# Hybrid DeltaNet / GLA / softmax layer on one core: GLA projections traced a pair ahead of the mixing, and a DeltaNet block inverse that is masked before its elimination

## The chip, the core and the metric

One NeuronCore of a Trainium2 chip runs the whole program. The metric is device time in microseconds (us), the median of several executions. Engines are named as in the profile: PE is TensorE (matmul), PEld its weight load, DVE is VectorE, ACT is ScalarE, POOL is GpSimd, SP is SyncE; a "q" behind a name is the engine's instruction queue issuing a DMA. Each engine works through its own list of instructions in order, so an instruction that waits holds up everything behind it on that engine.

## The reference, cut to what matters

A layer over 528 positions (16 meta tokens and 512 tokens) of width 2048: an RMS norm, one wide input projection, three token mixers on separate heads, an output projection, a residual sum and a last norm. The two mixers that the change touches:

```python
# gated DeltaNet, 6 heads of 128, chunks of 64; the kernel uses chunks of 128
a_mat = where(strict_lower, einsum(kb, kc) * decay, 0)
sol = triangular_solve(eye + a_mat, rhs)          # unit lower triangular
...
# GLA, 5 heads, key width 64: decay per key channel inside the score
attn = einsum('bhid,bhjd,bhijd->bhij', q_c, k_c, exp(g_i - g_j))   # i >= j
o = einsum(qd, s) + einsum(attn, v_c)
s = s * g_last + einsum(kd, v_c)
```

All of it is float32. Large matmuls split each operand into a rounded part and a remainder and sum three products.

## The kernel before

**The stream of projections.** `inproj` (L188) computes one block of 128 projection columns: two weight halves are loaded by SP, split by ACT (`whi`, L144) and DVE (`wlo`, L145), and each half feeds 48 matmuls of 264 or 258 columns or 24 of 512 (L174), with the two-deep buffers `raw`, `hi`, `lo`. The third product needs `wlo`, so DVE has to reach L145 before PE gets to the half. PE's 4368 such matmuls form one stream, in a fixed order, and everything else PE does is put between them.

**Who sets the order.** The program is traced in the order of the source, and a scheduler with a timeline of its own then orders every engine's list. Two things steer it by hand: `tc.high_priority(...)`, which moves what is traced inside ahead of what is ready at the same time (it is used for the weight splits, L143), and `behind(mm, n)` (L162), which ties a matmul behind the n-th projection matmul from the one last traced.

**DeltaNet.** For each group g of three heads (L885 to L892) the keys are projected (`dn_keys`), then values, queries, the inverse and the mixing. `dn_keys` forms the matrices `an` from `pg` (keys times keys), `e2` (the decays: DVE L434, ACT L435) and per-row factors (DVE L438). `dn_inverse` (L443) writes the 32-by-32 diagonal blocks of `an` through DRAM into `ab`, one block per partition (51 rows of 1024), eliminates with 60 DVE instructions (L463, L465), then selects the strict lower triangle and puts ones on the diagonal with two POOL instructions (L466, L468), and writes `ab` out (`sc`, L471) and back as `xc` (`iv`, L474), both issued by ACT. DVE transposes it (L479). PE then builds the inverse of the whole block in two steps: 32-row products `pm` and `pl` (L485, L494, L495) with copies by ACT (`m1` L489, `l1` L496) and DVE (`uf` L504), and 64-row products `pn` and `pu` (L515, L520). The first `pm` of each group is tied `PM[g]` = 308 or 310 projection matmuls behind the point where it is traced; `pn` has no tie.

**GLA.** `gla_pair` (L648) treats pair p (two heads for p = 0, 1, one for p = 2): it projects keys, queries and values, scans the log gates (`gu`, `gt`, `gc`; L669 to L676), computes the scores on eight levels of block size 64, 32, ..., 1, 0 (DVE L695 to L703, ACT L698, PE `pss` L717), copies them into place (L721, L725) or under a mask (DVE L729), and then runs the state and the output (`pkd` L742, `pg` L760, `pgn` L768, `pgo` L777, L783, `pgt` L797). PE writes `pss`, `pkd` and nearly all other small results to the four PSUM buffers of the tag "m"; a level's buffers come free when L721, L725 or L729 has read them. With two heads a level is 32 small matmuls (64 weight columns by 32), so two levels are a burst of 64.

Of the kernel before, what the change touches and what calls it, by code (L numbers as in the profile page):

```python
# [14 lines left out]
ALU = mybir.AluOpType  # L15
# [12 lines left out]
H = 3  # L28
# [49 lines left out]
def tile_hybrid_trunk(ctx, tc, xT, xtok, mtok, w_gate, w_in, w_out, consts, lmask, fin_w, out, dbg=None):  # L78
# [20 lines left out]
    V, A, G, PE = nc.vector, nc.scalar, nc.gpsimd, nc.tensor  # L99
# [62 lines left out]
    def behind(mm, n):  # L162

        later.append((mm.ins, len(order) + n))
# [85 lines left out]
    for b in range(5):  # L250
        r = NM if b == 4 else P
# [9 lines left out]
    for b in range(5):  # L261
        r = NM if b == 4 else P
# [55 lines left out]
    for k in range(KT):  # L318
        for xx in (xh, xl):
            for a in range(2):  # L320
                PE.matmul(pgate[a][:, :HT], wg[k // 8][:, k % 8, :], xx[k][:, a * HT : (a + 1) * HT],
                          start=(k == 0 and xx is xh), stop=(k == KT - 1 and xx is xl))
# [52 lines left out]
    def dn_keys(g):  # L375

        st = {}
        hs = range(H * g, H * g + H)
        kT = six.tile([P, H, T], F32, tag="six", name=f"kT{g}")
        for j, h in enumerate(hs):  # L380
            conv_silu(("dk", h), 6 + h, kT[:, j])
        gb = six.tile([P, H, T], F32, tag="six", name=f"gb{g}")
        nc.scalar.dma_start(out=gb, in_=gd[6 + H * g : 6 + H * g + H, :].partition_broadcast(P))
        kd = six.tile([P, NN, P], F32, tag="six", name=f"kd{g}")
        at = six.tile([P, NN, P], F32, tag="six", name=f"at{g}")
        an = six.tile([P, NN, P], F32, tag="six", name=f"an{g}")
        sk = wk.tile([P, 5, H], F32, tag="sk", name=f"sk{g}")
        kdm = t15(f"kdm{g}", (NM, H, P))
        anm = wk.tile([NM, H, NM], F32, tag="anm", bufs=1, name=f"anm{g}")
        atm = wk.tile([NM, H, NM], F32, tag="atm", bufs=1, name=f"atm{g}")  # L390
        cols = wk.tile([P, 4, 5, H], F32, tag="cols", name=f"cols{g}")
        nb2, br, nbg, tmp = (cols[:, i] for i in range(4))
        gcl = lambda b, j: gcol[:NM if b == 4 else P, b, 6 + H * g + j : 6 + H * g + j + 1]
        G.memset(sk, 1.0)
        for b in (4, 0, 1, 2, 3):
            r = NM if b == 4 else P
            ts = slice(0, NM) if b == 4 else bsl(b)
            pk = psm.tile([P, 512], F32, tag="m", name=f"pk{g}{b}")
            for j in range(H):
                PE.transpose(pk[:r, j * P : (j + 1) * P], kT[:, j, ts], ident)  # L400
            for j in range(H):
                sq = wk.tile([P, P], BF16, tag="sq", name=f"sqk{g}{b}{j}")
                A.activation(sq[:r], pk[:r, j * P : (j + 1) * P], AF.Square, accum_out=sk[:r, b, j : j + 1])
            e = at[:, b * H : b * H + H, :] if b < 4 else atm
            for j in range(H):
                V.tensor_scalar(e[:r, j, :], gb[:r, j, ts], gcl(b, j), 0.0, ALU.subtract, ALU.min)
            A.activation(e, e, AF.Exp)
            for j in range(H):
                dst = kd[:, b * H + j, :] if b < 4 else kdm[:, j, :]
                V.tensor_scalar_mul(dst, pk[:r, j * P : (j + 1) * P], e[:r, j, r - 1 : r])  # L410
            if b < 4:
                G.affine_select(out=e, in_=e, pattern=[[0, H], [1, P]], base=0, channel_multiplier=-1,
                                compare_op=ALU.is_ge, fill=0.0)
        A.activation(tmp, sk, AF.Ln, bias=eps_c)
        A.activation(br, tmp, AF.Exp, scale=-0.5)
        lb = gcol[:, :, H * g : H * g + H]
        gg = gcol[:, :, 6 + H * g : 6 + H * g + H]
        for sl, r in ((slice(0, 4), P), (slice(4, 5), NM)):
            c = lambda t: t[:r, sl, :]
            A.activation(c(tmp), c(lb), AF.Exp)  # L420
            V.tensor_tensor(out=c(nb2), in0=c(tmp), in1=c(br), op=ALU.mult)
            V.scalar_tensor_tensor(out=c(tmp), in0=c(nb2), scalar=-1.0, in1=c(br), op0=ALU.mult, op1=ALU.mult)
            V.tensor_copy(c(br), c(nb2))
            V.tensor_copy(c(nb2), c(tmp))
            A.activation(c(nbg), c(gg), AF.Exp)
            V.tensor_tensor(out=c(nbg), in0=c(nbg), in1=c(nb2), op=ALU.mult)
        for b in (4, 0, 1, 2, 3):
            r = NM if b == 4 else P
            ts = slice(0, NM) if b == 4 else bsl(b)
            pg = psm.tile([P, 512], F32, tag="m", name=f"pg{g}{b}")  # L430
            e2 = t15(f"e2{g}{b}")
            for j in range(H):
                PE.matmul(pg[:r, j * r : (j + 1) * r], kT[:, j, ts], kT[:, j, ts], start=True, stop=True)
                V.tensor_scalar(e2[:r, j, :r], gb[:r, j, ts], gcl(b, j), 0.0, ALU.subtract, ALU.max)  # L434
            A.activation(e2[:r, :, :r], e2[:r, :, :r], AF.Exp, scale=-1.0)  # L435
            for j in range(H):
                dst = an[:, b * H + j, :] if b < 4 else anm[:, j, :]
                V.scalar_tensor_tensor(out=dst, in0=pg[:r, j * r : (j + 1) * r], scalar=nb2[:r, b, j : j + 1],  # L438
                                       in1=e2[:r, j, :r], op0=ALU.mult, op1=ALU.mult)
        st.update(kT=kT, kd=kd, at=at, an=an, kdm=kdm, anm=anm, br=br, nbg=nbg)  # L440
        return st

    def dn_inverse(g, st):  # L443
        an, anm = st["an"], st["anm"]
        ab = six.tile([NN * 4 + H, 1024], F32, tag="six", name=f"ab{g}")
        G.memset(ab, 0.0)
        scr = drp.tile([NN * 4, 1024], F32, tag="scr", name=f"scr{g}", bufs=2)
        for r in range(4):
            nc.scalar.dma_start(
                out=scr.rearrange("(n r) (a c) -> r a n c", r=4, a=32)[r],  # L450
                in_=an[32 * r : 32 * r + 32, :, 32 * r : 32 * r + 32])
# [3 lines left out]
        nc.scalar.dma_start(  # L455
            out=ab[NN * 4 : NN * 4 + H, :].rearrange("h (a c) -> h a c", a=32)[:, 0:NM, 0:NM],
            in_=scm_.rearrange("a h c -> h a c"))
        a3 = ab.rearrange("p (a c) -> p a c", a=32)
        for j in range(1, 31):
            m = 31 - j  # L460
# [2 lines left out]
            V.tensor_tensor(out=t3, in0=a3[:, j + 1 :, j : j + 1].to_broadcast([NN * 4 + H, m, j]),  # L463
                            in1=a3[:, j : j + 1, 0:j].to_broadcast([NN * 4 + H, m, j]), op=ALU.mult)
            V.tensor_tensor(out=a3[:, j + 1 :, 0:j], in0=a3[:, j + 1 :, 0:j], in1=t3, op=ALU.add)  # L465
        G.affine_select(out=a3, in_=a3, pattern=[[1, 32], [-1, 32]], base=0, channel_multiplier=0,  # L466
                        compare_op=ALU.is_gt, fill=0.0)
        G.affine_select(out=a3, in_=a3, pattern=[[1, 32], [-1, 32]], base=0, channel_multiplier=0,  # L468
                        compare_op=ALU.not_equal, fill=1.0)
        sc2 = drp.tile([NN * 4 + H, 1024], F32, tag="sc2", name=f"sc2{g}", bufs=2)  # L470
        nc.scalar.dma_start(out=sc2, in_=ab)  # L471
        iv = six.tile([P, 4, NN, 32], F32, tag="six", name=f"iv{g}")
# [9 lines left out]
        for n in range(NN):  # L482
            for q in range(2):
                lo_, hi_ = slice(64 * q, 64 * q + 32), slice(64 * q + 32, 64 * q + 64)
                mm = PE.matmul(pm[lo_, n, :], an[hi_, n, lo_], uc[hi_, n, :], start=True, stop=True)  # L485
# [12 lines left out]
        uf = six.tile([P, NN, P], F32, tag="six", name=f"uf{g}")  # L498
# [6 lines left out]
        for q in range(2):  # L505
            ns = range(q * 6, q * 6 + 6)
            nsl = slice(q * 6, q * 6 + 6)
            b64 = t15(f"b64{g}{q}", (64, 6, 64))
            G.memset(b64, 0.0)
            V.tensor_copy(b64[0:32, :, 0:32], xc[0:32, nsl])  # L510
            V.tensor_copy(b64[32:64, :, 32:64], xc[32:64, nsl])
            V.tensor_copy(b64[32:64, :, 0:32], l1[32:64, nsl])
            pn = psm.tile([64, 6, 64], F32, tag="m", name=f"pn{g}{q}")
            for n in ns:
                PE.matmul(pn[:, n - q * 6, :], an[64:128, n, 0:64], uf[64:128, n, 64:128], start=True, stop=True)  # L515
            m2 = t15(f"m2{g}{q}", (64, 6, 64))
            A.copy(m2, pn)
            pu = psm.tile([64, 6, 64], F32, tag="m", name=f"pu{g}{q}")
            for n in ns:
                PE.matmul(pu[:, n - q * 6, :], b64[:, n - q * 6, :], m2[:, n - q * 6, :], start=True, stop=True)  # L520
            V.tensor_copy(uf[0:64, q * 6 : q * 6 + 6, 64:128], pu)
# [123 lines left out]

    kts, qts, ats = [], [], []

    def gla_pair(p):  # L648
        R = P if p < 2 else 64
        ne = 2 if p < 2 else 1  # L650
        qk = six.tile([P, 3, T], F32, tag="six", name=f"gqk{p}")
        kT, qT, gc = qk[:R, 0], qk[:R, 1], qk[:R, 2]
# [7 lines left out]
        vt = six.tile([P, 2, S], F32, tag="six", name=f"gvt{p}")  # L660
        vm = t15(f"gvm{p}", (NM, 2, P))
# [12 lines left out]
        A.activation(t, t, AF.Ln, bias=1.0)  # L674
        V.scalar_tensor_tensor(out=u, in0=u, scalar=0.0, in1=t, op0=ALU.min, op1=ALU.subtract)
        V.tensor_tensor_scan(gc, gsc[:R], u, 0.0, ALU.mult, ALU.add)  # L676
        SC = 1.0 / 16.0
        k4, q4, g4 = (a[:, NM:].rearrange("p (b t) -> p b t", b=NB) for a in (kT, qT, gc))
        n_n = ne * NB
# [220 lines left out]
    kts += [kq[0][:, :S], kq[0][:, S : 2 * S]]  # L900
    qts += [kq[0][:, 2 * S :], kq[1][:, :S]]
    ats.append(kq[1][:, S:].rearrange("p (n t) -> p n t", t=P))
    for p in range(3):
        gla_pair(p)
    for h in range(GLA_HEADS):
        dump(f"ogl{h}", zs["gz", h])
    for h in range(FOX_HEADS):
# [176 lines left out]
```

## Time and profile before

| | us |
|---|---|
| median of 3 runs | 1032.09 (1031.01 to 1033.81) |
| the profiled execution | 1035.39 |
| its span, first to last instruction | 1033.7 |
| PE busy in the span | 1011.4 (98%) |
| DVE, ACT, POOL busy | 566.7, 411.7, 136.4 |
| mean granted clock of PE in the span | 0.992 |

The profile's page gives busy time by engine, the chain of work that ended last, and groups of instructions by line. The waits of an engine list how long it stood idle and what ended the idle time. The table by stretches gives busy time inside chosen windows, with the granted clock of PE (PEclk, 1.00 is full speed). The timeline lists instructions with start, duration, engine, line and tile, and in brackets the idle time ahead of one and what ended it. A busy PE can still be a slow one, since a busy matmul at half the clock is busy too.

### The profile page before, as it was taken

What the parts mean: (1) busy time and instruction counts of PE and PEld (TensorE: products, weight loads), DVE (VectorE), ACT (ScalarE), POOL (GpSimd) and SP (SyncE); (2) the same over time, 40 slices, a digit from 0 to 9 for tenths busy, and PEclk for the clock granted to TensorE, in tenths of its full rate; (3) what the DMA queues carried; (4) which work ended last, traced back from release to release, by engine and by line L of the source; (5) the groups of instructions that cost most, each with busy time, mean ns of one, the idle gap of its engine ahead of it and who ended that gap; (6) DMA issues with size and microseconds to landing.
All of it is one profiled execution on the core that took longest, in us unless ns stands there. A gap on an engine that the chain in (4) does not pass through costs nothing.

```text
span 1033.7 us, 19032 instructions
## 1 busy us (share of the span) xinstructions
PE 1011.4 (98%) x7799; PEld 910.3 (88%) x7799; DVE 566.7 (55%) x1240; ACT 411.7 (40%) x899; POOL 136.4 (13%) x137
## 2 busy tenths in 40 slices
PE   9999999999999998999989999999999999999996
PEld 7899999989999888899989879898998988888885
DVE  6366868856577883243747474445454574423234
ACT  6644533343455343243444444343333353213223
POOL 0022212221122222100101010110101010000014
PEclk9999999999999998999999999999999999999998
DMA  9613232323222233132112122222232254222244
GB/s 354 239 62 115 83 90 91 102 78 108 78 83 81 78 102 99 49 94 74 62 48 83 44 92 66 91 82 92 82 93 82 93 193 133 82 100 85 102 142 163
DMA packets 42347, 105.15 MB, mean 102 GB/s; under 512 B 10589, under 2 KB 13917, under 8 KB 42260
## 3 DMA queue, kind: packets, MB, share of 16 engines
q1 hardware_dynamic: 28000, 92.33, 26.3%
q10 hardware_dynamic: 14260, 11.61, 4.1%
q8 instruction: 61, 1.00, 0.4%
q14 instruction: 26, 0.21, 0.1%
HBM read 98.74 MB, written 5.05 MB: 100 GB/s over the span
## 4 chain that ended last, share of the span: by engine, by line
PE 66%; DVE 5%; DMA 3%; issue 3%; ACT 2%; POOL 1%; ACTq 0%; POOLq 0%; DVEq 0%
PE pp L174 39%; PE pa L932 15%; DMA sc<-ab 1%; PE pss L717 1%; POOL stgz L294 1%; DVE wlo L145 1%; PE pfo L877 1%; PE pfa L845 1%; PE py L593 1%; PE pb L932 1%; PE pfx L860 1%; DVE ab L465 1%; PE po L608 1%; PE po L607 1%; PE pa L570 0%
## 5 line engine op out<-in xcount | busy, mean ns | idle before, releaser
L174 PE MATMUL pp<-xh,whi 128*128 128x264 f32 (+2 forms) x1456 | 378.2, 311 | 0.8 <-DVE vg L285 0.5
L174 PE MATMUL pp<-xl,whi 128*128 128x264 f32 (+2 forms) x1456 | 378.2, 311 | 0.0
L174 PE MATMUL pp<-xh,wlo 128*128 128x264 f32 (+2 forms) x1456 | 376.5, 310 | 0.0
L174 PEld LDWEIGHTS pp<-xh,whi 128*128 128x128 f32 x1456 | 244.4, 189 | 16.8 <-issue 3.1
L174 PEld LDWEIGHTS pp<-xl,whi 128*128 128x128 f32 x1456 | 245.6, 190 | 14.0 <-issue 1.0
L174 PEld LDWEIGHTS pp<-xh,wlo 128*128 128x128 f32 x1456 | 245.2, 190 | 13.1 <-issue 0.2
L145 DVE TENSOR_TENSOR wlo<-raw,whi 128x1024 fp32r<-128x1024 f32 x110 | 137.1, 1246 | 112.0 <-ACT whi L144 110.4
L144 ACT CAST whi<-raw 128x1024 fp32r<-128x1024 f32 x110 | 115.4, 1049 | 202.3 <-PE pp L174 175.3
L932 PE MATMUL pa<-wloo,oh 128*128 128x512 f32 x224 | 88.0, 393 | 0.0
L932 PE MATMUL pa<-whio,ol 128*128 128x512 f32 x224 | 87.9, 393 | 0.0
L932 PE MATMUL pa<-whio,oh 128*128 128x512 f32 x224 | 78.3, 396 | 0.0
L145 DVE TENSOR_TENSOR wloo<-rawo,whio 128x1024 fp32r<-128x1024 f32 x29 | 35.8, 1236 | 76.4 <-ACT whio L144 76.3
L144 ACT CAST whio<-rawo 128x1024 fp32r<-128x1024 f32 x29 | 30.4, 1049 | 83.8 <-PE pa L932 56.8
L932 PEld LDWEIGHTS pa<-whio,ol 128*128 128x128 f32 x224 | 42.2, 188 | 9.7
L932 PEld LDWEIGHTS pa<-wloo,oh 128*128 128x128 f32 x224 | 42.1, 188 | 9.4
L932 PEld LDWEIGHTS pa<-whio,oh 128*128 128x128 f32 x224 | 41.9, 188 | 9.2
L294 POOL TENSOR_SCALAR stc<-cv 128x528 f32<-128x528 f32 (+1 forms) x18 | 28.1, 1562 | 164.5 <-DVE cv L368 164.5
L368 DVE SCALAR_TENSOR_TENSOR cv<-pb,cpk,cv 128x528 f32<-128x528 f32 (+1 forms) x54 | 40.8, 756 | 0.8
L959 POOL TENSOR_TENSOR acc<-acc,fw 128x512 f32<-128x512 f32 x12 | 15.7, 1348 | 158.6 <-DMA fw<-in_fin_w 158.6
L285 DVE TENSOR_TENSOR pb<-pp,rstd 128x264 f32<-128x264 f32 (+1 forms) x36 | 13.8, 423 | 16.0 <-PE pp L174 15.9
L465 DVE TENSOR_TENSOR ab<-ab,ot 51x30 f32<-51x30 f32 (+14 forms) x60 | 21.4, 357 | 1.4
L463 DVE TENSOR_TENSOR ot<-ab 51x30 f32<-51x30 f32 (+14 forms) x60 | 20.1, 334 | 3.1 <-DMA ab<-scmeta 1.5
(384 smaller groups left out, 1279.8 us busy)
## 6 DMA issues: line engine op xcount, KB each, us to landing
raw<-in_w_in SPq DMA_DIRECT2D x110, 512.0 KB, 3.3
rawo<-in_w_out SPq DMA_DIRECT2D x29, 512.0 KB, 3.3
xt<-in_xtok SPq DMA_DIRECT2D x8, 512.0 KB, 9.9
acc<-in_xtok ACTq DMA_DIRECT2D x16, 256.0 KB, 5.2
out<-acc SPq DMA_DIRECT2D x16, 256.0 KB, 3.0
xs<-in_xT SPq DMA_DIRECT2D x7, 528.0 KB, 6.5
gb<-gd ACTq DMA_DIRECT2D x2, 792.0 KB, 7.4
eg<-gd ACTq DMA_DIRECT2D x8, 192.0 KB, 3.7
```

The lines of the kernel that those rows point to most:

```text
L144: A.copy(hi, raw)
L145: V.tensor_tensor(out=lo, in0=raw, in1=hi.bitcast(F32), op=ALU.subtract)
L174: mm = PE.matmul(p_[:, :nt], wt[:, j * m : (j + 1) * m], xx[k][:, t0 : t0 + nt], start=(k == 0 and wt is hi and xx is xh), stop=(k == KT - ...
L285: V.tensor_tensor(out=o, in0=p_[rows], in1=rstd[rows, t0 : t0 + n], op=ALU.mult)
L294: G.tensor_scalar_max(t, src, LOW)
L368: V.scalar_tensor_tensor(out=c, in0=pb[:, t0 + w : w + T], scalar=cwc[:, blk, w : w + 1], in1=c, op0=ALU.mult, op1=ALU.add)
L463: V.tensor_tensor(out=t3, in0=a3[:, j + 1 :, j : j + 1].to_broadcast([NN * 4 + H, m, j]), in1=a3[:, j : j + 1, 0:j].to_broadcast([NN * 4 + ...
L465: V.tensor_tensor(out=a3[:, j + 1 :, 0:j], in0=a3[:, j + 1 :, 0:j], in1=t3, op=ALU.add)
L593: PE.matmul(py[:, j * P : (j + 1) * P], uf[:, b * H + j, :], z[:, j, :], start=True, stop=True)
L607: PE.matmul(pj, at[:, b * H + j, :], y[:, j, :], start=True, stop=False)
L932: PE.matmul(p_, o_[:, s], w_, start=(first and n == 0), stop=(last and n == 2), **kw)
L959: G.tensor_tensor(out=acc[tb, cc], in0=acc[tb, cc], in1=fw[cc], op=ALU.mult)
```

## The change

Four edits. In `dn_keys` POOL zeroes the upper triangle of `e2`, so that `an` is strictly lower before it is written out. In `dn_inverse` the two selections behind the elimination go, and a memset puts ones on the diagonal of `ab` ahead of it. The first `pn` of group 0 is tied 380 projection matmuls (`PM[0] + 72`) behind the point of tracing. And `gla_pair` is cut into `gla_project` and `gla_mix`, traced as project 0, project 1, mix 0, project 2, mix 1, mix 2, the first two mixings with a raised priority.

```diff
@@ dn_keys
             A.activation(e2[:r, :, :r], e2[:r, :, :r], AF.Exp, scale=-1.0)
+            G.affine_select(out=e2[:r, :, :r], in_=e2[:r, :, :r], pattern=[[0, H], [-1, r]], base=0,
+                            channel_multiplier=1, compare_op=ALU.is_gt, fill=0.0)
             for j in range(H):
@@ dn_inverse
+        G.memset(ab[:, 0:1024:33], 1.0)
         a3 = ab.rearrange("p (a c) -> p a c", a=32)
...
-        G.affine_select(out=a3, in_=a3, pattern=[[1, 32], [-1, 32]], base=0, channel_multiplier=0,
-                        compare_op=ALU.is_gt, fill=0.0)
-        G.affine_select(out=a3, in_=a3, pattern=[[1, 32], [-1, 32]], base=0, channel_multiplier=0,
-                        compare_op=ALU.not_equal, fill=1.0)
...
-                PE.matmul(pn[:, n - q * 6, :], an[64:128, n, 0:64], uf[64:128, n, 64:128], start=True, stop=True)
+                mm = PE.matmul(pn[:, n - q * 6, :], an[64:128, n, 0:64], uf[64:128, n, 64:128],
+                               start=True, stop=True)
+                if g + n == 0:
+                    behind(mm, PM[g] + 72)
@@ gla_pair
-    def gla_pair(p):
+    def gla_project(p):
...
         V.tensor_tensor_scan(gc, gsc[:R], u, 0.0, ALU.mult, ALU.add)
+        return R, ne, kT, qT, gc, qk, vt, vm
+
+    def gla_mix(p, st):
+        R, ne, kT, qT, gc, qk, vt, vm = st
         SC = 1.0 / 16.0
@@ the trace
-    for p in range(3):
-        gla_pair(p)
+    gla = {0: gla_project(0), 1: gla_project(1)}
+    with tc.high_priority(offset=500):
+        gla_mix(0, gla[0])
+    gla[2] = gla_project(2)
+    with tc.high_priority(offset=500):
+        gla_mix(1, gla[1])
+    gla_mix(2, gla[2])
```

In the built program the lists change with it. Counted in projection matmuls that PE has issued before: `pm` of group 0 stays behind 1173, the first `pn` of group 0 goes from 1232 to 1245, `pm` of group 1 from 2143 to 2135, and the first `pn` of group 1 from 2192 to 2188. The scores of pair 0 start behind 2773 instead of 2675, and its three bursts of 64 have 25, 36 and 28 projection matmuls ahead of them instead of 15, 27 and 10; those of pair 1 have 31, 41 and 19 instead of 26, 24 and 16. The numbers of projection matmuls and of small matmuls are the same, the SP list is the same, and from the middle of the first softmax head on all lists are the same. In group 0, ACT now has the issue of `iv` (L474) ahead of the split of the half that starts at matmul 1152, and DVE has that half's `wlo` behind the transposes of L479; both were the other way round. In GLA, DVE's list holds the next pair's first levels and the next pair's gate work between the masked copies of a pair.

## The prediction

> **What bounds the kernel.** I read the page's head first, then PE's waits, then a table of stretches around each wait, then the timelines of the engines that PE waits for.
>
> ```profile
> PE 1011.4 (98%) x7799; PEld 910.3 (88%) x7799; DVE 566.7 (55%) x1240; ACT 411.7 (40%) x899; POOL 136.4 (13%) x137
> ```
>
> PE is busy 1011.4 of 1033.7 us, so it is the bound, and the change removes no PE work. What it can win is PE's idle time, 22.3 us in all, of which about 8 lie behind the last matmul, and time at a lowered clock. PE's waits:
>
> ```profile
> PE pss L717 <- issue: 3.5, 3, 1.4
> PE pm L485 <- DVE iv L479: 3.0, 1, 3.0
> PE pn L515 <- DVE uf L504: 2.3, 1, 2.3
> ...
> PE pkd L742 <- DVE a L729: 1.1, 1, 1.1
> ```
>
> The columns are total us, times, longest. All of the large ones stand in code that the change touches. The stretches around them (length; busy us of PE, PEld, DVE, ACT, POOL; PEclk):
>
> ```profile
> 231.00:238.00 7.00, 5.80 (x42) 5.57 (x43) 5.25 (x12) 2.73 (x4) 0.00 (x0) 0.76 0.26 77
> ...
> 403.00:411.00 8.00, 7.77 (x72) 6.91 (x72) 3.16 (x6) 4.02 (x7) 0.00 (x0) 0.57 0.19 66
> ...
> 510.00:532.00 22.00, 18.82 (x539) 16.95 (x539) 15.09 (x42) 7.73 (x15) 2.80 (x3) 1.00 0.22 73
> ...
> 563.00:585.00 22.00, 19.59 (x549) 17.79 (x548) 14.77 (x42) 7.68 (x14) 3.77 (x3) 1.00 0.22 75
> ```
>
> Behind the `pn` wait the clock is 0.76 over 7 us, so (1 - 0.76) x 7 = 1.7 us are lost; behind the `pm` wait it is 0.57 over 8 us, 3.4 us lost. With the waits the two places cost 2.3 + 1.7 = 4.0 us and 3.0 + 3.4 = 6.4 us. The scores of pairs 0 and 1 cost 3.2 and 2.4 us of idle PE at full clock, and pair 2 (623 to 640 us) another 0.5: 6.1 in all.
>
> [...]
>
> **Selections out of the chain.** The chain of group 0 on POOL, ACT and DVE:
>
> ```profile
> 205.58 1.26 POOL L466 TENSOR_SCALAR_AFFINE_SELECT ab<-ab 51x1024 f32<-51x1024 f32 x1 [7.44 <-issue]
> 206.91 1.55 POOL L468 TENSOR_SCALAR_AFFINE_SELECT ab<-ab 51x1024 f32<-51x1024 f32 x1
> ```
>
> ```profile
> 208.49 0.26 ACTq L471 DMA_DIRECT2D sc<-ab  x1
> 211.70 1.05 ACT L144 CAST whi<-raw 128x1024 fp32r<-128x1024 f32 x1 [4.81 <-PE pp L174]
> 215.15 0.40 ACTq L474 DMA_DIRECT2D iv<-sc  x1
> 215.57 1.53 ACTq L476 DMA_DIRECT2D xm<-sc  x1
> ```
>
> ```profile
> 212.78 1.23 DVE L145 TENSOR_TENSOR wlo<-raw,whi 128x1024 fp32r<-128x1024 f32 x1 [0.97 <-ACT whi L144]
> 219.67 0.58 DVE L479 STREAM_TRANSPOSE iv<-iv 128x384 f32<-128x384 f32 x1 [5.66 <-DMA iv<-sc]
> ```
>
> DVE's last elimination ends at 205.45 and `sc` is issued at 208.49, so 3.0 us go from the chain; in group 1 it is 390.10 to 392.80, 2.7 us. What is added: the diagonal memset waits for the landing of `ab`, but DVE's list waits for it only at the fourth step, so I cost it at nothing (0 to 0.4 us, DVE's step of 0.20 and its wait). The ten selections on `e2`: the nearest row is L412, same shape, 0.52 us alone. They stand ahead of L438, which in group 1 starts at 334.97, 3.3 us after the last decays leave ACT (331.6), so they are hidden; five masked products instead of three then stand behind a `wlo` at 339.25, two more of 0.28 = 0.6 us later for `scr`. DVE's later waits for ACT in the chain (1.1, 0.9 and 1.0 us ahead of L298) absorb that: I take 0.2 us, range 0 to 0.6.
>
> **Group 0.** `pm` stays behind matmul 1173, which PE reaches at 220.05; `uc` was ready at 220.25, so `pm` gains nothing. `pn` goes 13 matmuls back. A stretch of 90 such matmuls in the chain takes 11.21 us, 0.125 each, so that is 1.6 us of cover. The rest comes from upstream: `l1` (ACT L496, 230.78) is behind the three ACT steps of a conv block whose POOL step ended at 228.7; that order stays, so without the edit at `pn` the wait would stay. Replayed with the durations above, `uf` is ready near 230.9 and PE comes to `pn` at 232.4 (pl's end, moved to 226.4 by the next paragraph, plus 48 x 0.125): no wait, and 4.0 us won.
>
> **A wait is added there.** ACT now issues `iv` before it splits the half that PE starts at matmul 1152 (217.5 by count), and DVE's `wlo` of that half stands behind L479. `sc` issued at 205.5 lands 6.64 us later (208.49 to 215.13), `iv` is issued at 212.2 and lands 4.5 us later, at 216.7; the transposes and two copies take until 217.8 (219.67 to 220.80 before) and `wlo` until 219.0. PE needs it four matmuls into the half, at 218.0. So PE stalls about 1.0 us where it did not before. Net 3.0 us; between 1.3 (the stall trips the clock, 1.7) and 4.0.
>
> **Group 1.** `pm` comes 8 matmuls (1.0 us) earlier, at 399.1. `sc` at 390.2 lands at 396.8, and `iv` was covered before: DVE took it up at 402.60, behind L298, so it needed at most 3.1 us from 399.48; group 0's took 4.5. With 2.9 us it lands at 399.8, transposed at 400.4: `pm` waits 1.3 us. Then ACT has four copies (L502, 2.07 us), an activation, a split and another activation ahead of `m1` (L489), which ends near 405.7, while PE comes to `pl` at 404.8: 0.9 us more. Both are short of the 2.3 us that lowered the clock, so 6.4 - 2.2 = 4.2 us are won. With 4.5 us for `iv`, the first wait is 2.9 us, the clock drops as before, and 0.3 us are left. Range 0 to 6.
>
> **GLA.** DVE replayed through its new list with start-to-start steps from 504 to 528 us (0.34 us for L695 to L703, 0.60 for two L721, 1.2 for four L725, 0.40 for two L729, 1.14 for `wlo`, 1.2 for the scan): pair 0's level 1 is 0.3 us late, and `pkd` finds its PSUM buffer 1.4 us late, since L729 of level 1 now stands behind three levels of pair 1. Pair 1: 0.6 and 2.4 us. Pair 2: 0.5. That is 5.2 us. The "issue" waits (3.5 us) come in the middle of a burst of 64 when no data is missing; three of six bursts had one. I keep half, 1.7, bounded by 0 and 3.5. So 6.9 against 6.1: 0.8 us lost; from 6.1 won to 5 lost.
>
> **Sum.** 3.0 + 4.2 - 0.8 - 0.2 = 6.2 us off the profiled 1035.4, 1029.2. That execution lies 3.3 us above the median shown, so in medians 1032.1 - 6.2 = **1025.9**.
>
> **Rivals.** *One: the DMA stays the limit in group 1.* `iv` takes 4.5 us as in group 0, `pm`'s wait is 2.9 us and the clock falls. For it: group 0's row. Against: 402.60 - 399.48 in group 1. Then 3.0 + 0.3 - 0.8 - 0.2 = 2.3 won: 1029.8. *Two: the scores flow.* With more projection matmuls between bursts all 6.1 us of GLA go: 7.2 - 0.2 + 6.1 = 13.1, 1019. For it: the spacings; against: DVE is busy 15.1 of 22 us there and gets more work. *Three, slower: DVE becomes the bound of GLA.* The next pair's levels wait for their exponentials on ACT inside DVE's list (an L698 is 0.63 us, a split 1.05), so that each pair's `pkd` waits 4.4 us and each wait lowers the clock (1.7): 3 x 6.1 + 1 for late levels = 19.3 against 6.1, less 7.0 won before, so 6 us lost: 1038. It decides from 13 us of GLA idle on, a `pkd` wait of 2.3 us with its clock loss in all three pairs. Pair 1's 2.4 us stands at that edge.
>
> [...]
>
> **Chances.** Forecast 0.52 (1021 to 1028.5), rival one 0.20, rival two 0.13, rival three 0.15. Up to 0.3% (3.1 us, 1029.0 to 1035.2) a change can't be told from none. Rival one straddles that: a quarter of it counts as faster. Faster 0.52 + 0.13 + 0.05 = 0.70; same 0.15 plus 0.04 of rival three = 0.19; slower 0.11. The range leaves out half of rival two below and two thirds of rival three above: 1019 to 1033.
>
> **What would show it.** Right: no `pn` wait and clock 1.00 behind 232; a `pp` stall near 1 us ahead of the first `pm`, with `wlo` as its releaser; `pm` of group 1 waits 1 to 2 us at full clock; `pkd <- a` grows to 3 to 4 us while "issue" shrinks. Wrong: a clock below 1.00 near 403, or PE idle over 10 us between 498 and 660.

## The result and the profile after

The changed kernel takes 1030.45 us (median of 21 runs, 1028.39 to 1033.13) beside 1033.19 for the kernel before (21 runs): a ratio of 0.9973, 95% interval 0.9965 to 0.9982. That is 2.7 us faster, where 6.2 were forecast. The profiled executions stand further apart, 1035.39 and 1030.72, and part of what follows is why.

The page's engines, and its DMA queues of the kind "instruction" (packets, MB, share of 16 engines):

```profile
PE 1010.8 (98%) x7799; PEld 910.6 (88%) x7799; DVE 564.7 (55%) x1240; ACT 412.2 (40%) x899; POOL 129.1 (13%) x145
...
q8 instruction: 61, 1.00, 0.4%
```

PE's waits (total us, times, longest):

```profile
PE pss L723 <- issue: 2.9, 1, 2.9
PE pm L484 <- DVE iv L478: 2.0, 1, 2.0
PE pp L174 <- issue: 1.9, 1, 1.9
...
PE pkd L748 <- DVE a L735: 0.3, 1, 0.3
```

The stretches around the same places (length; busy PE, PEld, DVE, ACT, POOL; PEclk):

```profile
228.00:235.00 7.00, 7.00 (x63) 6.79 (x62) 3.74 (x10) 2.85 (x4) 0.00 (x0) 1.00 0.24 77
395.00:403.00 8.00, 5.98 (x78) 5.73 (x77) 2.43 (x6) 5.55 (x10) 2.68 (x3) 0.79 0.17 27
526.00:542.00 16.00, 13.53 (x340) 12.68 (x340) 14.37 (x40) 5.54 (x12) 0.00 (x0) 1.00 0.26 77
577.00:592.00 15.00, 11.86 (x308) 11.00 (x308) 9.82 (x30) 8.35 (x16) 2.89 (x3) 0.89 0.12 38
```

Group 0 is clean: no `pn` wait, clock 1.00. In group 1 `pm` still waits 2.0 us and the clock is 0.79 over 8 us (1.7 lost). In GLA the many short waits have become two long ones, both put down to "issue", and the second lowered the clock (0.89 over 15 us, 1.7 lost). DVE, which I expected to be late there, ends almost none of PE's idle time: `pkd` waits 0.3 us where I had 1.4 and 2.4.

Following the ACT weight splits, which occur in both traces in the same order, the lead of the changed kernel is -0.8 us at 210 us (start-up), 3.2 us behind group 0, 5.7 behind group 1, and 4.8 behind GLA: in these two executions 4.0 and 2.5 us are won and 0.9 lost.

### The profile page after: what moved, and what is told of

Read it like the earlier page. It is cut to its first block, busy times and chain, and to the rows that moved or that the text cites. A ratio compares the mean times of both kernels' runs of the same rounds, so it can differ in the third digit from the quotient of the medians.

```text
span 1029.0 us, 19034 instructions
## 1 busy us (share of the span) xinstructions
PE 1010.8 (98%) x7799; PEld 910.6 (88%) x7799; DVE 564.7 (55%) x1240; ACT 412.2 (40%) x899; POOL 129.1 (13%) x145
## 4 chain that ended last, share of the span: by engine, by line
PE 87%; DVE 6%; DMA 2%; ACT 2%; issue 1%; POOL 1%; ACTq 0%; SPq 0%; DVEq 0%; POOLq 0%
PE pp L174 54%; PE pa L943 16%; PE pp L227 4%; DVE wlo L145 1%; POOL stgz L294 1%; PE pgate L321 1%; PE pfo L883 1%; PE pfa L851 1%; DMA sc<-ab 1%; PE pss L723 1%; DVE ab L468 1%; PE pg L433 1%; PE py L595 1%; PE pb L943 1%; DVE ot L466 1%
## 5 line engine op out<-in xcount | busy, mean ns | idle before, releaser
L145 DVE TENSOR_TENSOR wlo<-raw,whi 128x1024 fp32r<-128x1024 f32 x110 | 135.5, 1232 | 102.9 <-ACT whi L144 101.2
```

The lines of the kernel that those rows point to most:

```text
L145: V.tensor_tensor(out=lo, in0=raw, in1=hi.bitcast(F32), op=ALU.subtract)
```

## The experiments

All comparisons are with runs of the kernel before on the same chip, made together with them.

**The two edits apart.** Theory A, from the two traces, has the DeltaNet edits win about 5 us and GLA lose 1 to 3; rival B lets the GLA edit cost nothing. `dn_only` is the changed kernel with the pairs traced as before, `gla_only` the opposite:

```diff
-    gla = {0: gla_project(0), 1: gla_project(1)}
...
+    for p in range(3):
+        gla_mix(p, gla_project(p))
```

> The DeltaNet edits alone (masks ahead of the elimination, pn tied), the GLA pairs traced as before. Theory A, from the two traces: what is won is 4.0 us in group 0 (the pn wait of 2.3 us and 1.7 us at half clock) and 1.0 us of the pm wait of group 1, and the clock is lowered or not from run to run, since it is granted in stretches of 3.41 us whose start is not tied to the program; so 3.3 to 6.7 us faster, about 5. The prediction's steps: 3.0 + 4.2 - 0.2 = 7.0 us faster. Rival B, the GLA edit costs nothing and the DeltaNet edits bring the whole: 2.7 us faster, as in the changed kernel.

> The GLA edit alone (projections a pair ahead), DeltaNet as before. Theory A: the scores wait for PE's own instructions, which arrive by DMA 256 at a time, and with the weight loads between them they arrive later than before; 1 to 3 us slower, with PE's waits for issue at pss 4 to 6 us in total and none of them ended by DVE. The prediction's steps: 0.8 us slower, with 4.4 us of waits of pkd for the masked copies. Rival B: no difference within 0.5 us.

`dn_only`: 1028.33 us, 0.9953 (0.9940 to 0.9967), 4.8 us faster. `gla_only`: 1036.23 us, 1.0031 (1.0016 to 1.0047), 3.1 us slower. Rival B falls: the change is two edits of opposite sign. PE's waits of `dn_only`:

```profile
PE pss L723 <- issue: 2.9, 3, 1.1
PE pkd L748 <- DVE a L735: 1.5, 2, 1.2
...
PE pm L484 <- DVE iv L478: 1.0, 1, 1.0
PE pl L493 <- ACT iv L488: 0.8, 2, 0.5
```

and its group 1:

```profile
394.00:404.00 10.00, 8.20 (x190) 7.45 (x189) 3.42 (x7) 7.03 (x12) 2.80 (x3) 1.00 0.23 51
```

This is the forecast of group 1: 1.3 and 0.9 us of waits were expected, 1.0 and 0.8 came, at full clock. PE's waits of `gla_only`:

```profile
PE pm L485 <- DVE iv L479: 3.3, 1, 3.3
PE pss L721 <- issue: 3.1, 1, 3.1
PE pn L515 <- DVE uf L504: 2.4, 1, 2.4
PE pp L174 <- issue: 1.6, 1, 1.6
```

DeltaNet waits as before, and GLA has the same two long waits for issue as the changed kernel. They add up to 4.7 us; three half-clock windows of 3.41 us in GLA add 5.1 us. Between the same two weight splits on either side of GLA (484.9 and 690.4 us in the trace before), PE is idle for 6.4 us before, 5.6 in the changed kernel and 5.1 in `gla_only`, while the time lost at half clock there is 0, 1.7 and 5.1 us. So the GLA edit loses no time in waits as such. What it loses is clock, behind fewer and longer waits. Over all runs the same shows: the median clock is 0.991 in the 12 runs of `gla_only` and 0.994 in the 29 runs before, which is 3.1 us of the span.

**The DeltaNet edits apart.** `tie_only` adds to the kernel before only the tie of the first `pn`; `sel_only` has only the moved masks.

```diff
+                if g + n == 0:
+                    behind(mm, PM[g] + 72)
```

> Before, with the tie of the first pn of group 0 alone. Theory A: the pn wait goes without the masks being moved, since 13 matmuls are 1.6 us and group 0 has nothing else late: 1.6 to 4.0 us faster, and pm of group 1 waits 3 us as before. The prediction's step: 1.6 of the 2.3 us of wait are covered and 0.7 us stay, without a lower clock: 3.3 us faster. Rival: without the earlier inverse the wait comes back whole behind the 13 matmuls: no difference.

> Before, with the masks moved ahead of the elimination and no tie at pn. The prediction's step: in group 0 the wait of pn stays, since l1 stands behind three ACT steps of a conv block, and group 1 wins 4.2 us. Theory A: group 1 wins 1.0 us of wait and at most 1.7 us of clock, and group 0 little: 1 to 3 us faster, with a wait of pn of 1 to 2.3 us. Rival: the earlier inverse alone removes the wait of pn too, and the tie brings nothing: as fast as the DeltaNet edits together.

`tie_only`: 1031.49 us, 0.9978 (0.9965 to 0.9991). The wait of `pn` is as forecast, 0.7 us left:

```profile
PE pm L485 <- DVE iv L479: 3.1, 1, 3.1
...
PE pn L515 <- DVE uf L504: 0.8, 1, 0.8
```

`sel_only`: 1027.81 us, 0.9950 (0.9932 to 0.9969), as fast as both together, and without any `pn` wait. The rival holds and my step does not: I had `l1` (230.78 before) stay behind three ACT steps of a conv block. The order did stay, but the whole row moved (L495 is `l1` here):

```profile
226.29 0.65 ACT L295 ACTIVATE stc<-stc 128x528 f32<-128x528 f32 x1 [2.84 <-POOL stc L294]
226.97 0.65 ACT L296 ACTIVATE stc<-stc 128x528 f32<-128x528 f32 x1
227.65 0.65 ACT L297 ACTIVATE stc<-stc 128x528 f32<-128x528 f32 x1
228.32 0.48 ACT L495 COPY iv<-pl 128x384 f32<-128x384 f32 x1
```

The POOL step that these wait for had ended at 228.7 and now ends at 226.3, since its inputs come from DVE, behind the transposes (219.67 before, 215.30 here). Given the earlier inverse, the tie buys nothing that these runs can tell.

**What "issue" is.** The page has 61 packets of 1.00 MB on an instruction queue: 16 KB each. PE's 7799 matmuls and 7799 weight loads, divided by 61, are 256 a packet (`shift64` below, with 128 pairs more, has 62 packets). So PE's program arrives while it runs, 128 pairs of load and matmul at a time; a burst of 64 small float32 matmuls is shown as 128 pairs, one whole packet. PE around the first long wait of the changed kernel, and behind the second:

```profile
529.34 0.40 PE L174 MATMUL pp<-xh,whi 128*128 128x264 f32 x2
529.88 1.06 PE L723 MATMUL pss<-kq 64*32 64x32 f32 x64
530.86 0.92 PE L723 MATMUL pss<-kq,kq 64*32 64x32 f32 x64
533.71 0.51 PE L174 MATMUL pp<-xl,whi 128*128 128x264 f32 x2 [1.94 <-issue]
...
585.72 0.26 PE L723 MATMUL pss<-gqk 64*32 64x32 f32 x6 [2.92 <-issue]
```

and all that DMA moved from 530.5 to 533.5 (40 slices of 0.075 us):

```profile
GB/s 0 0 0 0 0 0 0 0 0 0 218 0 0 0 0 0 0 0 0 0 0 0 0 0 0 0 0 0 0 0 0 0 0 0 0 0 0 0 0 0
DMA packets 1, 0.02 MB, mean 5 GB/s; under 512 B 0, under 2 KB 0, under 8 KB 0
...
q8 instruction: 1, 0.02, 2.0%
```

One packet, started at 531.32 and landed at 532.28 by its record; PE goes on 1.43 us later. The same holds for all 21 waits for issue of 0.5 us or more in the traces of this case: each ends 1.3 to 1.6 us behind the landing of such a packet, and, counted in PE's matmul records, 79 to 86 records behind a multiple of 128. So each of them stands at the border of a packet; waits for data end at no fixed place. Since 512 KB of weights moved just ahead of it, theory C said that fetches wait behind weight loads, and theory D that it doesn't matter what the DMA carries or where the packets begin. `few_bytes` shrinks the loads of the GLA blocks (it loads one slice of 128 columns in eight and repeats it, and leaves the other seven out), `shift64` moves the packets' borders, `after_spread` and `after_spread48` pull the bursts apart:

```diff
+        if name in FEW:
+            nc.sync.dma_start(out=raw[:, :128], in_=src[:, :128])
+            r8 = raw[:, :128].unsqueeze(1).to_broadcast([P, 8, 128])
```

```diff
+    for i in range(64):
+        PE.matmul(pw[:32, :32], ones[:32, :32], ones[:32, :32], start=True, stop=True)
```

```diff
+    AT = (2773, 3006, 0)
+    STEP = (40, 40, 0)
...
+                        if li % 2 == 0 and b + r + e == 0 and AT[p]:
+                            later.append((mm.ins, AT[p] + li // 2 * STEP[p]))
```

> The changed kernel, but the weight halves of the GLA blocks and of the first softmax head's keys and values load 64 KB instead of 512 KB (one slice of 128 columns, repeated by the split, so the other seven slices are left out); every engine's list stays the same but for these shapes. Theory C, PE's instruction fetches wait behind weight loads on the DMA: the fetches that came 4.5 to 5.3 us after they were due come after 1 to 2.5 us, PE's waits for issue in GLA fall from 4.8 us to under 2 us without a half-clock stretch there, and the kernel is 3 to 5 us faster than the changed one, 1025.5 to 1027.5. Theory D, the fetch or PE's own rate of issue is the limit whatever the DMA carries: waits of 4 to 5 us stay, 1030.

> The changed kernel with 64 more 32-by-32 matmuls behind the warm-up at the start, which move the borders of the 256-instruction fetches by half a fetch against the bursts and change nothing else in the order. Theory C: the waits for issue in GLA move to other matmuls of the bursts, or shrink or grow by 1 us or more. Theory D, a burst of 64 small matmuls is itself slower to issue than to run, or data is late: they stay at the same matmuls (the last third of pair 0's third burst and pair 1's last level) with the same lengths. Time: 0.5 to 1 us for the matmuls, and between 2 us less and 2 us more by theory C.

> The changed kernel with every second score level of pairs 0 and 1 tied, so that pair 0's bursts of 64 have 40, 40 and 40 projection matmuls ahead of them (25, 36 and 28 before), and pair 1's are pulled apart in the same way as far as its buffers let it. Theory C: 128 matmuls then take at least 6.2 us, longer than the slowest fetch (5.3 us and 1 us to land), so that the waits for issue of pair 0 go, and of pair 1 mostly; 3 to 5 us faster than the changed kernel, 1025.5 to 1027.5. Theory D: each burst of 64 still waits as long, 1030. Prediction's reason, DVE is late: pkd and pss wait for the masked copies either way, and nothing is won.

> As the one with 40, but 48 projection matmuls between the levels' ties. Theory C: pair 0 wholly free of waits for issue; pair 1 has 33, 35 and 23 between its bursts, and pair 2's last two bursts stand together ahead of one block's end, so one wait of 1 to 2 us is left there; 1026 to 1028. Theory D: 1030.

`few_bytes`: 1029.86 us, 0.9962 (0.9948 to 0.9975), and the waits for issue stay, 2.7 us at `pss` and 2.5 at `pp`. From 524.7 to 532.7, with next to no weights on the DMA:

```profile
DMA packets 145, 0.08 MB, mean 10 GB/s; under 512 B 16, under 2 KB 144, under 8 KB 144
...
q1 hardware_dynamic: 144, 0.07, 2.8%
q8 instruction: 1, 0.02, 0.7%
```

The fetch still starts only at 530.39, behind the same burst. Theory C falls. (The 4.5 to 5.3 us of the expectation are theory C's reckoning; counted from PE's entry into the packet ahead, the two fetches that PE waited for in the changed kernel started 1.4 and 2.6 us later.)

`shift64`: 1033.37 us, 1.0005 (0.9990 to 1.0020), waits at the same matmuls. That was no test: the 64 matmuls are 128 pairs, exactly one packet, so the borders came to lie where they were. Its time has another reason: in the profiled run the 64 matmuls take PE from 5.2 to 10.3 us, the clock is at half from 7.9 to 14.8 us, and the run is 5.3 us behind the changed kernel at 80 us. Three other traces have 3.4 us of half clock in the start-up too (the changed kernel's has none), so how much of it the 64 matmuls bring is not settled.

`after_spread`: 1024.96 us, 0.9914 (0.9897 to 0.9930), with no wait for issue left:

```profile
PE pm L484 <- DVE iv L478: 2.1, 1, 2.1
PE pkd L750 <- DVE a L737: 1.3, 2, 0.8
...
PE pss L723 <- DVE kq L709: 1.1, 2, 0.6
```

`after_spread48`: 1029.38 us, 0.9961 (0.9945 to 0.9976). It has no wait for issue either, but pairs 1 and 2 are pushed later, and the first softmax head waits:

```profile
PE pp L174 <- DVE fqk L285: 2.5, 1, 2.5
PE pss L723 <- DVE kq L709: 1.9, 3, 0.9
```

Two half-clock windows behind these waits (623.4 and 650.7) cost 3.4 us more. So spacing is worth it up to the point where the work behind becomes late.

**Where the borders lie.** From the four traces theory E: PE asks for a packet when it enters the one ahead of it, and can use it about 3.8 us later (529.88 to 533.71). If the packet that it enters is one burst, it is through in 1.9 us and waits 1.9. (The expectation speaks of the fetch after next; by these times it is the next one, since the wait ends behind the landing of the fetch that started inside the burst.) `shift32` moves the borders by half a packet in the changed kernel; `spread_shift54` moves a border onto the head of a burst in `after_spread`:

```diff
+    pad = psm.tile([P, 512], F32, tag="m", name="pad")
+    for i in range(32):
+        mm = PE.matmul(pad[:32, :32], ones[:32, :32], ones[:32, :32], start=True, stop=True)
+        if i == 0:
+            behind(mm, 0)
```

> The changed kernel with 32 small matmuls more ahead of GLA (after 2754 projection matmuls; 64 instruction pairs, half a fetch), the order otherwise unchanged. Theory E, from the traces so far: PE's instructions come in fetches of 256 (128 pairs of weight load and matmul; a small float32 matmul is two pairs, so a burst of 64 is just one fetch); the fetch after next is asked for when PE enters a fetch, and takes about 3.8 us to be usable whatever the weight loads do; a burst that lies wholly in one fetch runs in 1.2 to 1.7 us, so PE waits 2 us behind it. In the changed kernel pair 0's second and pair 1's last burst lie so; half a fetch on, each fetch holds 19 or more projection matmuls and the waits for issue (4.8 us) go to under 1 us, with no half-clock stretch in GLA: 1025 to 1028 us. Rival, the bursts are slow to issue wherever they lie: 1030.5 to 1031.

> The kernel with pair 0's and 1's score levels pulled apart, which had no wait for issue, with 54 small matmuls more ahead of GLA (108 pairs), so that the border of a fetch falls on the first matmul of pair 0's third group of 64, 40 projection matmuls behind the second. Theory E: PE waits 2 to 2.5 us for issue right behind that burst, lowers its clock there in about half of the runs, and waits for issue nowhere else in pair 0; 2.5 to 4 us slower than without the 54, 1027.5 to 1029. Rival, spacing alone decides: no wait there and 0.5 to 0.8 us more for the 54 matmuls, 1025.5.

`shift32`: 1028.98 us, 0.9967 (0.9950 to 0.9985). The mechanism is right: all 4.8 us of waits for issue are gone. The time is not, for two reasons. The 32 matmuls have a price: they take PE from 486.9 to 489.5 us, half clock follows from 490.0 to 493.4, and over this stretch the trace falls 3.9 us behind that of the changed kernel, of which it wins back 2.4 in GLA. And DVE is late next:

```profile
PE pkd L748 <- DVE a L735: 3.8, 2, 2.2
...
PE pss L723 <- DVE kq L709: 0.5, 1, 0.5
```

The packets' phase and DVE were two limits one behind the other, of nearly equal size: 4.8 and 3.8 us.

`spread_shift54`: 1027.05 us, 0.9950 (0.9935 to 0.9965), slower than `after_spread`, whose interval lies below. But the time says nothing for theory E: the 54 matmuls take PE from 488.7 to 492.7 us, over them the trace falls 3.8 us behind that of `after_spread`, and behind that the distance stays at 4.2 us up to the end of GLA. That the time came out slower, as forecast, is luck. What bears on theory E is the wait. It stands right behind the burst that was put on a border, and at no other burst of pair 0:

```profile
536.71 0.76 PE L723 MATMUL pss<-kq,kq 64*32 64x32 f32 x64
538.03 0.40 PE L174 MATMUL pp<-xh,wlo 128*128 128x264 f32 x2 [0.57 <-issue]
```

The place is as forecast; the size is 0.6 us, not 2 to 2.5, and no time is lost by it that the weight splits show. The packet's record starts at 535.58, ahead of the burst (536.10), where in the changed kernel it started 1.4 us into it. So theory E holds for the place, but the moment at which a packet is asked for is not always the entry of its matmul. In the changed kernel the operand of the burst came from DVE at 529.74, 0.14 us ahead of it. That PE reads its instructions ahead of the matmuls, and that this lead was gone there, is my guess; no run shows it.

**Both mended.**

```diff
-    PM = (308,310)
+    PM = (308,330)
```

> The kernel with the score levels pulled apart, and the tie of the first pm of group 1 moved 20 matmuls back (PM = 308, 330; pm comes behind 2155 projection matmuls instead of 2135). By the traces the wait of pm in group 1, 0.7 to 2.1 us from run to run, and its half-clock stretch go, since 20 matmuls are 2.5 us; 1 to 3 us faster than without, 1022 to 1024. Rival: the chain behind pm (pl, uf, pn) comes later and waits in its place: 1025.

`best` (`after_spread` with this line): 1022.91 us, 0.9913 (0.9891 to 0.9934). The `pm` wait is gone, and PE waits for a weight split there instead:

```profile
PE pp L174 <- ACT whi L144: 1.1, 1, 1.1
...
PE pp L174 <- DVE wlo L145: 0.5, 1, 0.5
```

By the ratios it isn't told apart from `after_spread`. Both beat the changed kernel and `dn_only`, clear of the intervals.

## Why the prediction was wrong

The sign and the DeltaNet mechanism were right; the size was not: 2.7 us against 6.2, just under half. Two terms were mis-sized.

*GLA: -0.8 us forecast, -3.1 measured in `gla_only` (1.0031, interval 1.7 to 4.9 us); the ratios of `dn_only` and the changed kernel differ by 2.1 us.* The step that failed was "I keep half, 1.7, bounded by 0 and 3.5" for the waits for issue, together with a clock loss in GLA that the sum put at nothing. I took a wait that the profile ascribes to nothing as a fixed cost of dense bursts, halved by wider spacing. It is the program's own fetch, and 4.8 us of it were left, as two waits of 1.9 and 2.9 us in place of three of 1.0 to 1.4. The packets that PE had run through ahead of these waits are nearly all scores in both kernels (118 to 123 of 128 matmul records before, 128 and 122 in the changed one). What differs is when the next fetch starts: 0.6 and 0.9 us behind PE's entry before (in the third, 2.7, PE waited for data meanwhile), 1.4 and 2.6 us in the changed kernel. Why it starts later is open. PE's idle time in GLA did not grow by it (6.4 us before, 5.6 in the changed kernel), but longer single waits lowered the clock: by 1.7 us in the traces of the changed kernel, `few_bytes` and `shift64`, by 5.1 in that of `gla_only`, and by nothing in the four traces without the GLA edit (`before`, `dn_only`, `tie_only`, `sel_only`). That the two profiled executions lose 0.9 us in GLA where 0.8 were forecast is luck, since neither part of the forecast came.

The other part of the step, 1.4 + 2.4 = 3.8 us of `pkd` behind the masked copies, is not in the trace of the changed kernel (0.3 us), and it is in that of `shift32`, as 1.6 + 2.2: it was there, hidden behind the fetch. Waits on one path that overlap don't add; the later counts.

*The median: 7.0 us for DeltaNet, 4.8 measured.* By profiles the step holds: 1035.39 to 1027.96 for `dn_only` is 7.4 us. What failed is "so in medians 1032.1 - 6.2". The profiled execution lost 5.1 us to half clock behind its two waits, which most runs do not lose in full: its clock was 0.992, and the median of 29 runs of the kernel before is 0.994, 2.1 us less. 1035.39 lies 2.2 us above the median of those runs, 1027.96 lies 0.4 below that of `dn_only`. One can't take 6.2 us off a median that has not got them. The median of three runs, 1032.1, was also 1.1 us below that of the 21 runs.

One sum of the prediction is off without moving the forecast: rival one leaves 6.4 - 2.9 - 3.4 = 0.1 us of group 1, not 0.3.

The smaller steps. *Group 0:* the wait and the clock went, 4.0 us. The `wlo` stall of 1.0 us did not come: `sc` took 4.9 us from issue to landing (206.32 to 211.24), not 6.6, and `iv` 3.8, not 4.5. The price of a DMA was read from one sample each. *The tie* is right by itself (0.8 us left, 0.7 forecast) and without use beside the masks. *Group 1:* 1.0 + 0.8 us at full clock in `dn_only`, as forecast; in the profiled run of the changed kernel `sc` took 7.5 us and `pm` waited 2.0 with the clock down, which is rival one in part: the DMA was the limit, but by `sc` and not by `iv`. *Rival three* had the right sign for GLA and DVE as its cause; the cause was another. *Rival two* had the right remedy: with enough projection matmuls between the bursts the scores do flow, but it needed ties.

**The clock.** Between the first and the last matmuls, every half-clock stretch lasts 3.41 us or a multiple, and all of one run begin on one grid of that step, which lies differently in each run: in the trace before they begin at 232.73 and 403.40 us, 50 steps of 3.413 us apart, in that of the changed kernel at 398.99 and 586.72, 55 steps apart, and counted from the first instruction the two grids lie 2.4 us apart. I laid the grid over the traces of 13 kernels and took PE's idle time in each of its windows behind the start-up. Of the windows at full clock with 2.0 us or more idle, 10 of 10 were followed by a half-clock stretch; of 14 with 1.2 to 2.0 us, 4; of 46 with 0.5 to 1.2 us, none. The wait of 1.94 us at 531.8 in the changed kernel fell across a border (0.3 and 1.6) and cost no clock; that of 2.0 us at 396 lay in one window and did. Idle time is not the whole rule: the window ahead of the half clock at 490.0 in `shift32` has none, but 2.7 us of the added 32x32 matmuls, and that ahead of 7.9 in `shift64` likewise 2.7 us of them; two windows of `spread_shift54` with 2.2 and 1.9 us of them cost no clock. So a wait of 2 to 3 us costs 1.7 us more in some runs and nothing in others. Over 21 runs of the changed kernel, time follows clock loss (span x (1 - clock)) with a slope of 0.8 and a correlation of 0.84.

What stays open: when exactly a fetch is asked for, and whether PE reads ahead of its matmuls; the wait behind a burst on a border was 1.9 us in one kernel and 0.6 in another. The added waits of the `e2` selections (0.2 us) were not measured by themselves.

## What to carry to other kernels

Before an "issue" wait on PE is priced, count PE's instructions in the stretch against the packets of the instruction queue: in this case 128 pairs that ran in less than about 4 us could wait for the next packet (3.2 to 5.0 us from entry to use where the waits were over 1 us and nothing else held PE up), and which bursts did depended on where the packets began, so an edit ahead of them could move it (32 matmuls in `shift32` took all 4.8 us of these waits away); with 40 large matmuls between bursts 0.6 us of wait was left when a border lay on the head of one (`spread_shift54`). Small matmuls put in to move the packets had a price of their own, 3.9 us for 32 of them. Price a wait of 2 us or more with the clock as a chance (1.7 us in 10 of the 10 windows that held 2.0 us of idle time, none behind the 1.94 us that fell across a border), and take it off a median only with that chance. Of two waits on one path, add the longer, not both (`pkd` waited 0.3 us behind the fetch and 3.8 without it).

## What the runs showed of the hardware that was not expected

PE's instructions came in 16 KB packets, 256 at a time, in 0.9 to 2.6 us each, and at the waits PE went on 1.3 to 1.6 us behind the landing. Consecutive fetches started no closer than 3.3 us. The clock fell after 2.0 us idle in a window of 3.41, and in `shift32` after a window without idle time that held 2.7 us of 32x32 matmuls. The start-up of one and the same code ran at full clock in nine traces; in three the clock fell to half for 3.4 us between 8.7 and 13.0 us.
